# The MLPs of a two-layer hybrid encoder step: another order of the first up products, another order of the down products, resident weight halves loaded in steps

## The chip, the cores and the metric

The kernel runs on one core of a Trainium2 chip. The metric is the device time of one execution in microseconds (us); lower is better. A core has five engines that work at the same time, each through its own instructions in its own order, and wait for one another by semaphores: TensorE (PE in the profile, its weight loads PEld) for matrix products, VectorE (DVE), ScalarE (ACT) and GpSimd (POOL) for elementwise work, and SyncE (SP), which here only issues transfers (DMA) between the chip's memory (DRAM) and SBUF, the larger of the core's two on-chip memories. Products accumulate in the smaller one, PSUM, in banks. DMAs are issued from SP's queue and from POOL's queue.

## The reference, cut to what matters

The program is one inference step of a small encoder with two layers (`DEPTH = 2`, `D_MODEL = 1024`), over 1072 tokens: 16 meta tokens, 32 sample frames and 1024 prompt frames. Each layer has a mixer (attention and gated linear attention in layer 0, forgetting attention in layer 1) and then an MLP with a hidden width of 4096. The change touches the MLPs:

```python
def mlp(h, w_up, w_down):
    u = jax.nn.relu(h @ w_up)
    return (u * u) @ w_down
...
        xp = xp + mlp(rmsnorm(xp, norm_mlp[l]), w_up[l], w_down[l])
        xs = xs + mlp(rmsnorm(xs, norm_mlp[l]), w_up[l], w_down[l])
```

Everything is fp32.

## The kernel before

**fp32 as three products.** Each fp32 operand is split into a high part (a cast on ACT, line 64) and a low part (the rest, a subtraction, line 66 on DVE or line 68 on POOL, by the last argument of `hi_lo`). `mm3` then issues three products: high x high (line 75), high x low (76), low x high (77). In the profile a wait at line 75 is thus one for a high part, a wait at 76 one for the low part of the activations, a wait at 77 one for the low part of the weights.

**Seven products instead of eight.** Both matrix products of an MLP are done by a Strassen-Winograd scheme: each matrix is cut into 2 x 2 quadrants, and seven products of sums of quadrants make the result. The names are those of the scheme: A11, A12, A22, S1 to S4 are weights (S: sums of quadrants), B11, B21, B22, T1 to T4 activations (T: sums of quadrants). T1 is B12 - B11; T2 is B22 less T1 and needs T1 first; T3 is B22 - B12; T4 is B21 - T2.

**Layout.** `xT` holds the residual in SBUF, transposed: 128 partitions x 8 blocks of features x 1072 tokens. The tokens are cut into four quarters (`qs`) of 268 (layer 0) or 264 (layer 1). Quarters 0 and 1 are the left halves of B (B11: feature blocks 0 to 3, B21: 4 to 7), quarters 2 and 3 the right ones (B12, B22). One column index `c` (0 or 1) says which quarter of a half is meant, so a T1 of column 1 needs quarters 1 and 3.

**The norm ahead of it.** `mlp_norm(q)` normalizes quarter `q`: eight squares on ACT (134) with sums on DVE and POOL (136, 139), the mean over features as a product with a constant matrix (`normed`, 145), a Newton step (148 to 152) to 1/sqrt, and then eight multiplications in place, one for each feature block (878). `norm(cols, between)` issues the squares, then the steps handed in as `between`, then the rest, mean product included. `mlp_sums(q)` (884 on) then forms T1, T2, T3, T4 and B22 of this column, each with its high and low part into an `ho_` tile (`operand`). It is called for quarter 2 and, behind `mlp_norm(3)`, for quarter 3.

**The up product** (`up`) is a generator, one step a `yield`. It runs over 16 pairs `b` (a pair is 128 hidden units from either half) and, inside, over the seven products of `UP`: A11, A12, S1, S2, S3, A22, S4. A step makes two outputs (`c` = 0, 1) of 12 products each: 24 products. `ready(at)` makes the weights of four steps ahead: `up_load` loads a pair's raw weights (two DMAs of 512 KB into `mu_raw`, two buffers), `up_weights` forms sums and splits them into `mu_w` (five buffers). Results of a pair go, squared-ReLU and differences included (994, 1001, 1005), into eight slots laid over one half of `xT`, the halves taken in turn by even and odd pairs. Pair 0 keeps its first sum in `mu_early`, since `xT` is still being read at that time. When a pair is done, one DMA from POOL's queue stores seven of its slots to DRAM (`ud`, in four tiles of four pairs each; 1008). The last pair's store is kept back (`last_store`, 1093) until the down product has begun. `mlp` hands two up steps to `mlp_norm(3)` as `between`.

**The down product** (`down`) runs seven products of `DOWN` (`n`), each in two passes (`c`), each pass over 16 blocks `kb` of 12 products. `acts` loads the activations of two pairs from `ud` (SP's queue, 1067; three buffers `md_ur`) and splits them into `md_u` (four buffers), three groups ahead. `weights(n, kb)` makes the weights of a block in `md_w{kb}`, one buffer each, which is refilled in the pass `c` = 1 of the product before. Two halves of `w_down` quadrants stay in SBUF as `k1` and `k2`, 16 blocks each in four tiles of 1 MB; other quadrants are loaded block by block into `md_raw` (256 KB each, three buffers). Before the change, `k1` is loaded with A11 ahead of the first pass from SP's queue, and `k2` with A21 during the first pass, at blocks 2, 6, 10 and 14, from POOL's queue; each of these loads stands behind a one-element copy (`behind`, 1073) that waits for the activations of its block. S2 = A21 + A22 - A11 is the second product, so its weights (1041, 1042, then the split) are made during the second pass. At block 4 of the first four products the residual of the product's quadrant is loaded back into `xT` from `xsave` (1121, POOL's queue), and at the end of a pass the outputs in PSUM are added to it (1139). A product starts new sums in PSUM if `n` is in `first`; the others go on in the sums of the product before.

**What sets the order.** In `mlp` PE's order is that of the program (`manual_schedule` for PE), and in `down` the orders of SP and POOL are, too, up to the second product. All else, DVE and ACT throughout, is ordered by a planner that simulates the time line when the kernel is built.

## Time and profile before

| | us |
|---|---|
| time before, median of 3 runs | 2821.92 |
| the runs | 2826.71, 2821.92, 2815.38 |
| the profiled execution, its own time | 2817.04 |
| its span (first to last instruction) | 2815.3 |
| its mean granted TensorE clock | 0.969 of full speed |

The profile is of one execution; its span is 1.7 us shorter than the time of that execution. A row of its first part gives an engine's busy time, share of the span and count of instructions. Rows of the order in time give start, duration, engine, line, operation, what is written and what is read, and in brackets how long the engine was idle before and what ended the idling. Rows in which instructions are merged give their count as x2, x4 and so on. Rows of the waits give the time waited in all, how many times, and the longest wait. Rows of stretches give the bounds, the length, the busy time and count of PE, PEld, DVE, ACT and POOL, then the granted PE clock, the busy share of the DMA engines and GB/s. The MLP of layer 0 has its up product from 582 to 934 us and its down product from 934 to about 1285; that of layer 1 from 2102 to 2451 and from there to the end.

### The profile page before, as it was taken

The numbers are of one execution on the slowest core, as the hardware profiler recorded it, in microseconds if no ns is written. First come the engines' busy times: TensorE is split into PE (matmuls) and PEld (weight loads), VectorE is DVE, ScalarE is ACT, GpSimd is POOL, SyncE is SP. The second block draws the span as 40 slices with busy tenths as digits, with TensorE's granted clock in tenths as the row PEclk, the third lists the DMA queues.
The fourth block names the chain that finished last, engine by engine and source line by source line (L and its number), as shares of the span: only waits on it lengthen the run. The fifth ranks groups of instructions, "written<-read, shape, count | busy, mean of one in ns | idle before, by whom it ended". The sixth has DMA issues, their size and how long they took to land.

```text
span 2815.3 us, 49213 instructions
## 1 busy us (share of the span) xinstructions
PE 2624.8 (93%) x18391; PEld 2437.4 (87%) x18391; DVE 1892.2 (67%) x3850; ACT 1266.0 (45%) x2833; POOL 634.5 (23%) x693
## 2 busy tenths in 40 slices
PE   5899999869999999999999888999968999999998
PEld 5888988769999899998798766778868999999998
DVE  5934478786766686677634556778788767677553
ACT  4345465443333354545333356666653333335342
POOL 3423365110000211012201244555510000111000
PEclk9999999989999999999999989999989999999999
DMA  6343242225443766544464555444232344586643
GB/s 194 101 134 105 74 149 58 75 87 160 128 155 128 279 207 202 145 132 130 131 207 134 145 144 133 98 101 98 63 92 96 130 154 141 180 269 210 195 142 104
DMA packets 358038, 394.82 MB, mean 140 GB/s; under 512 B 41567, under 2 KB 294200, under 8 KB 355752
## 3 DMA queue, kind: packets, MB, share of 16 engines
q1 hardware_dynamic: 340840, 306.55, 38.2%
q0 software_dynamic: 16960, 85.13, 8.4%
q8 instruction: 145, 2.38, 0.4%
q14 instruction: 93, 0.76, 0.1%
HBM read 264.99 MB, written 125.48 MB: 139 GB/s over the span
## 4 chain that ended last, share of the span: by engine, by line
PE 75%; DVE 11%; DMA 4%; ACT 2%; issue 2%; POOL 1%; SPq 0%; DVEq 0%; ACTq 0%; POOLq 0%
PE bank L75 12%; PE bank L76 12%; PE bank L77 12%; PE mu_y L76 8%; PE mu_y L77 8%; PE mu_y L75 8%; PE bank L1490 3%; PE bank L1500 2%; PE bank L1501 1%; DMA md_ur<-ud 1%; PE fx_s L1472 1%; PE fx_s L1473 1%; PE bank L257 1%; DMA md_raw<-in_w_down 1%; DVE xT L878 1%
## 5 line engine op out<-in xcount | busy, mean ns | idle before, releaser
L75 PE MATMUL bank<-pj_wh,h 128*128 128x384 f32 (+3 forms) x832 | 300.1, 363 | 9.8 <-ACT pj_wh L64 7.4
L77 PE MATMUL bank<-pj_wh,h 128*128 128x384 f32 (+3 forms) x832 | 297.4, 359 | 6.1 <-DVE h L66 4.8
L76 PE MATMUL bank<-pj_wl,h 128*128 128x384 f32 (+3 forms) x832 | 298.5, 360 | 3.0 <-DVE pj_wl L66 2.9
L76 PE MATMUL mu_y<-md_u,md_w 128*128 128x268 f32 (+1 forms) x896 | 259.9, 290 | 13.3 <-DVE md_u L66 11.3
L77 PE MATMUL mu_y<-md_u,md_w 128*128 128x268 f32 (+1 forms) x896 | 259.4, 290 | 6.1 <-POOL md_w L68 6.1
L75 PE MATMUL mu_y<-md_u,md_w 128*128 128x268 f32 (+1 forms) x896 | 260.7, 291 | 0.3 <-ACT md_u L64 0.2
L75 PE MATMUL bank<-md_u,md_w 128*128 128x268 f32 (+1 forms) x896 | 257.3, 287 | 0.0
L76 PE MATMUL bank<-md_u,md_w 128*128 128x268 f32 (+1 forms) x896 | 255.9, 286 | 1.2 <-DVE md_u L66 1.2
L77 PE MATMUL bank<-md_u,md_w 128*128 128x268 f32 (+1 forms) x896 | 255.6, 285 | 0.0
L64 ACT CAST md_u<-md_ur 128x536 fp32r<-128x536 f32 (+1 forms) x224 | 141.6, 636 | 232.0 <-PE mu_y L77 119.6
L66 DVE TENSOR_TENSOR md_u<-md_ur,md_u 128x536 fp32r<-128x536 f32 (+1 forms) x220 | 155.3, 710 | 131.3 <-ACT md_u L64 131.1
L77 PE MATMUL mu_y<-ho_T,mu_w 128*128 128x268 f32 (+1 forms) x768 | 220.0, 286 | 0.0
L76 PE MATMUL mu_y<-ho_T,mu_w 128*128 128x268 f32 (+1 forms) x768 | 219.8, 286 | 0.0
L75 PE MATMUL mu_y<-ho_T,mu_w 128*128 128x268 f32 (+1 forms) x768 | 219.3, 286 | 0.0
L1303 POOL TENSOR_TENSOR fx_p<-fx_p,sm_den 128x144 f32<-128x144 f32 (+7 forms) x128 | 150.6, 1177 | 182.1 <-DVE sm_den L1302 166.6
L66 DVE TENSOR_TENSOR mu_w<-mu_raw,mu_w 128x512 fp32r<-128x512 f32 x160 | 109.6, 687 | 116.9 <-ACT mu_w L64 116.9
L76 PEld LDWEIGHTS mu_y<-md_u,md_w 128*128 128x128 f32 x896 | 172.4, 192 | 15.2 <-DVE md_u L66 12.8
L64 ACT CAST mu_w<-mu_raw 128x512 fp32r<-128x512 f32 x160 | 99.3, 622 | 190.6 <-PE bank L77 124.7
L75 PEld LDWEIGHTS bank<-pj_wh,h 128*128 128x128 f32 x832 | 160.2, 193 | 22.8 <-ACT pj_wh L64 7.9
L77 PEld LDWEIGHTS mu_y<-md_u,md_w 128*128 128x128 f32 x896 | 172.3, 192 | 6.5 <-POOL md_w L68 6.5
L77 PEld LDWEIGHTS bank<-pj_wh,h 128*128 128x128 f32 x832 | 159.8, 192 | 17.6 <-DVE h L66 5.1
L76 PEld LDWEIGHTS bank<-pj_wl,h 128*128 128x128 f32 x832 | 160.3, 193 | 15.9 <-DVE pj_wl L66 4.4
(553 smaller groups left out, 8156.4 us busy)
## 6 DMA issues: line engine op xcount, KB each, us to landing
md_raw<-in_w_down SPq DMA_DIRECT2D x160, 256.0 KB
mu_raw<-in_w_up SPq DMA_DIRECT2D x64, 512.0 KB
ud<-xT POOLq DMA_DIRECT2D x16, 1876.0 KB, 7.5
md_ur<-ud SPq DMA_DIRECT2D x112, 268.0 KB
ud<-xT POOLq DMA_DIRECT2D x16, 1848.0 KB, 10.0
md_ur<-ud SPq DMA_DIRECT2D x112, 264.0 KB
fh_ka<-zk SPq DMA_DIRECT2D x32, 260.0 KB
md_k<-in_w_down SPq DMA_DIRECT2D x8, 1024.0 KB
```

Source lines behind the costliest of these rows:

```text
L64: nc.scalar.copy(hi, src)
L66: nc.vector.tensor_tensor(lo, src, hi.bitcast(F32), op=ALU.subtract)
L75: mm(out, ah, bh, start=start, stop=False)
L76: mm(out, ah, bl, start=False, stop=False)
L77: mm(out, al, bh, start=False, stop=stop)
L257: nc.tensor.matmul(*args, start=k == x == 0, stop=k == KB - 1 and x == 1)
L878: nc.vector.scalar_tensor_tensor(x[:, k], x[:, k], self.gain[:, 2 * self.l + 1, k:k + 1], y, op0=ALU.mult, op1=ALU.mult)
L1303: nc.gpsimd.tensor_tensor(p[:, :n], p[:, :n], den[:, 0:1].to_broadcast([P, n]), op=ALU.mult)
L1472: nc.tensor.matmul(s[:, a:b], qa[:, qc], ka[:, t0 + a:t0 + b], start=True, stop=False)
L1473: nc.tensor.matmul(s[:, a:b], qb[:, qc], kb[:, t0 + a:t0 + b], start=False, stop=ma >= mb)
L1490: nc.tensor.transpose(pt[:m, P * j:P * j + P], pr[j][:, k0:k0 + m], self.ident)
L1500: nc.tensor.matmul(po[:, c], vt[:m, t], th[:m, c], start=t == 0, stop=False)
```

## The change

In the up product the order of steps starts with A11 and A12 of pair 0, then A11 and A12 of pair 1; then come the other five products of pair 0, then those of pair 1, then the pairs from 2 on as before. Pair 1 gets a `mu_early` of its own. `mlp` hands four steps instead of two to `mlp_norm(3)`. T1's difference and split move into a function `first_sum`, which for quarter 3 is issued behind the fourth of the eight multiplications of `mlp_norm`. `nm_t` has three buffers instead of four, but for the first norm of the program.

In the down product A12 comes first and A11 second; the rest keeps its order. `k2` is loaded first, with A12; `k1` gets A11 during the first product and `k2` gets A21 during the second, at the blocks listed in `later`, from POOL's queue behind the same kind of copy. So S2's weights are made one product later. The low parts at the start are all on DVE. Weights are made four blocks ahead instead of six in the first pass. Of the last pair, the square, the four differences and the store are issued one at a time in the first blocks of the first pass. The residual is loaded at block 6, and for the products 0, 2, 3 and 4.

```diff
--- before.py
+++ after.py
@@ -130,7 +130,7 @@
             e = at in (1, 3, 5)
             first = at < 2
             at += 1
-            sq = acc[e] if first else sb.tile([P, QMAX], F32, name="nm_t", bufs=4)[:, :w]
+            sq = acc[e] if first else sb.tile([P, QMAX], F32, name="nm_t", bufs=3)[:, :w]
             nc.scalar.activation(sq, x[:, k], AF.Square)
             if not first:
                 (nc.gpsimd if e else nc.vector).tensor_tensor(acc[e], acc[e], sq, op=ALU.add)
@@ -213,7 +213,7 @@
         few = TILES[0][1] if first else 0
         for k in range(KB):
             g = self.gain[:, n, k:k + 1]
-            t = sb.tile([P, w], F32, name="nm_t", bufs=4)[:, :w - few]
+            t = sb.tile([P, w], F32, name="nm_t", bufs=3 if n else 4)[:, :w - few]
             nc.vector.scalar_tensor_tensor(t, x[:, k, few:], g, y[:, few:], op0=ALU.mult, op1=ALU.mult)
             self.hi_lo(t, hi[:, k, few:], lo[:, k, few:], "g" if k % 2 else "v")
         if few:
@@ -876,9 +876,18 @@
         x = self.xT[:, :, c0:c1]
         for k in range(KB):
             nc.vector.scalar_tensor_tensor(x[:, k], x[:, k], self.gain[:, 2 * self.l + 1, k:k + 1], y, op0=ALU.mult, op1=ALU.mult)
+
+            if q == 3 and k == 3:
+                self.first_sum(q)
         if q < 2:
             for n, name in enumerate(("B11", "B21")):
                 self.operand(name, x[:, 4 * n:4 * n + 4], q)
+
+    def first_sum(self, q):
+        (a0, a1), (c0, c1) = self.qs[q - 2], self.qs[q]
+        b11, b12 = self.xT[:, 0:4, a0:a1], self.xT[:, 0:4, c0:c1]
+        self.nc.vector.tensor_tensor(b11, b12, b11, op=ALU.subtract)
+        self.operand("T1", b11, q)
 
 
     def mlp_sums(self, q):
@@ -886,8 +895,8 @@
         (a0, a1), (c0, c1) = self.qs[q - 2], self.qs[q]
         b11, b21 = (self.xT[:, k:k + 4, a0:a1] for k in (0, 4))
         b12, b22 = (self.xT[:, k:k + 4, c0:c1] for k in (0, 4))
-        sub(b11, b12, b11)
-        self.operand("T1", b11, q)
+        if q == 2:
+            self.first_sum(q)
         sub(b11, b22, b11)
         self.operand("T2", b11, q)
         sub(b12, b22, b12)
@@ -942,10 +951,12 @@
         slot = {x: n + 1 for n, x in enumerate(self.STORED)}
         slot["B12"] = 0
         tt, stt = nc.vector.tensor_tensor, nc.vector.scalar_tensor_tensor
-        todo = [(b, n) for b in range(self.NP) for n in range(7)]
+
+        todo = [(b, n) for b in range(2) for n in range(2)] + [(b, n) for b in range(2) for n in range(2, 7)]
+        todo += [(b, n) for b in range(2, self.NP) for n in range(7)]
         pairs, ws = {}, {}
 
-        early = sb.tile([P, hw], F32, name="mu_early", bufs=1)
+        early = [sb.tile([P, hw], F32, name=f"mu_early{b}", bufs=1) for b in range(2)]
         self.ud = [self.dram.tile([P, 4, 7, hw], F32, name=f"ud{self.l}{g}") for g in range(4)]
 
         def ready(at):
@@ -974,7 +985,7 @@
                 for k in range(4):
                     self.mm3(out, (w[:, 0, k], w[:, 1, k]), (act[:, 0, k, cc], act[:, 1, k, cc]), first and k == 0, k == 3, wn in ("S2", "S3", "A22", "S4"))
                 u = {x: y[:, cc] for x, y in v.items()}
-                u1 = early[:, cc] if b == 0 else u["B11"]
+                u1 = early[b][:, cc] if b < 2 else u["B11"]
                 if wn == "A11":
                     nc.scalar.copy(u1, out)
                 elif wn == "A12":
@@ -994,26 +1005,25 @@
                 stt(x, src, 0.0, src, op0=ALU.max, op1=ALU.mult)
 
             if wn == "S1":
-                squared(v["B11"], early if b == 0 else v["B11"])
+                squared(v["B11"], early[b] if b < 2 else v["B11"])
             elif wn == "S3":
                 squared(v["B22"], v["B22"])
             elif wn == "A22":
                 tt(v["B21"], v["B21"], v["B21"], op=ALU.mult)
             elif wn == "S4":
-                squared(v["B12"], v["B12"])
+                self.last = [partial(squared, v["B12"], v["B12"])]
                 for x, p, m in (("T1", "B12", "B11"), ("T2", "B22", "T1"), ("T3", "B22", "B12"), ("T4", "B21", "T2")):
-                    tt(v[x], v[p], v[m], op=ALU.subtract)
-                store = partial(nc.gpsimd.dma_start, self.ud[b // 4][:, b % 4], place[:, b % 2, 1:8, :hw])
-                if b < self.NP - 1:
-                    store()
-                else:
-                    self.last_store = store
+                    self.last.append(partial(tt, v[x], v[p], v[m], op=ALU.subtract))
+                self.last.append(partial(nc.gpsimd.dma_start, self.ud[b // 4][:, b % 4], place[:, b % 2, 1:8, :hw]))
+
+                while b < self.NP - 1 and self.last:
+                    self.last.pop(0)()
                 del pairs[b]
             yield
 
 
-    DOWN = (("A11", "B11", ("11",)), ("S2", "T2", ("12",)), ("S3", "T3", ("22",)), ("A22", "T4", ("21",)),
-            ("A12", "B21", ("11",)), ("S1", "T1", ("22", "12")), ("S4", "B22", ("12",)))
+    DOWN = (("A12", "B21", ("11",)), ("A11", "B11", ("11",)), ("S2", "T2", ("12",)), ("S3", "T3", ("22",)),
+            ("A22", "T4", ("21",)), ("S1", "T1", ("22", "12")), ("S4", "B22", ("12",)))
 
 
     def down(self, k1, k2, sb, ps, mid, done):
@@ -1037,6 +1047,8 @@
             a, b = (k[kb // 4][:, kb % 4] for k in (k1, k2))
             if x == "A11":
                 src = a
+            elif x == "A12":
+                src = b
             elif x == "S2":
                 tt(b, b, raw("A22", kb), op=ALU.add)
                 tt(b, b, a, op=ALU.subtract)
@@ -1065,7 +1077,7 @@
             t = sb.tile([P, 2, QMAX], F32, name="md_ur", bufs=3)[:, :, :qw]
             hl = sb.tile([P, 2, 2, QMAX], F32R, name="md_u", bufs=4)[:, :, :, :qw]
             nc.sync.dma_start(t, self.ud[g // 2][:, 2 * (g % 2):2 * (g % 2) + 2, s, qw * c:qw * c + qw])
-            self.hi_lo(t, hl[:, 0], hl[:, 1], "g" if (n, c) == (0, 0) and g < 2 else "v")
+            self.hi_lo(t, hl[:, 0], hl[:, 1])
             return hl
 
 
@@ -1084,18 +1096,20 @@
 
         order = ExitStack()
         order.enter_context(self.tc.manual_schedule(engines={mybir.EngineType.SP, mybir.EngineType.Pool}))
-        load(k1[0], "A11", 0, 4)
+        load(k2[0], "A12", 0, 4)
         ready(0)
         for x in range(1, 4):
-            load(k1[x], "A11", 4 * x, 4)
-        for kb in range(6):
-            w[0, kb] = weights(0, kb, "g" if kb < 3 else "v")
-        self.last_store()
+            load(k2[x], "A12", 4 * x, 4)
+
+        later = {(0, 0, 10): (k1[0], "A11", 0), (0, 0, 14): (k1[1], "A11", 4), (0, 1, 2): (k1[2], "A11", 8), (0, 1, 6): (k1[3], "A11", 12),
+                 (1, 0, 4): (k2[0], "A21", 0), (1, 0, 8): (k2[1], "A21", 4), (1, 0, 12): (k2[2], "A21", 8), (1, 1, 0): (k2[3], "A21", 12)}
+        for kb in range(4):
+            w[0, kb] = weights(0, kb)
         at = 0
         out = {}
         for n, c in passes:
             x, _, to = self.DOWN[n]
-            first = n in (0, 4, 5, 6)
+            first = n in (0, 1, 5, 6)
             if (n, c) == (1, 0):
                 order.close()
             if first:
@@ -1105,14 +1119,17 @@
                     ready(at)
                     u = us.pop(todo[at])
                     at += 1
-                if n == 0 and c == 0 and kb + 6 < NP:
-                    w[0, kb + 6] = weights(0, kb + 6)
-                if n == 0 and c == 0 and kb % 4 == 2:
-                    x = k2[kb // 4]
+                if n == 0 and c == 0 and kb + 4 < NP:
+                    w[0, kb + 4] = weights(0, kb + 4)
+
+                if self.last:
+                    self.last.pop(0)()
+                if (n, c, kb) in later:
+                    x, name, k = later[n, c, kb]
                     behind(x[0:1, 0, 0:1], u)
-                    load(x, "A21", kb - 2, 4, nc.gpsimd)
-
-                if n < 4 and kb == 4:
+                    load(x, name, k, 4, nc.gpsimd)
+
+                if n in (0, 2, 3, 4) and kb == 6:
                     c0, c1 = self.qs[2 * (int(to[0][1]) - 1) + c]
                     f = 4 * (int(to[0][0]) - 1)
                     for k in range(f, f + 4, 2):
@@ -1122,7 +1139,7 @@
                 for ob in range(4):
                     f = slice(P * ob, P * ob + P)
                     hl = w[n, kb]
-                    self.mm3(out[c][ob], (hl[:, 0, f], hl[:, 1, f]), (u[:, 0, kb % 2], u[:, 1, kb % 2]), first and kb == 0, kb == NP - 1, n in (1, 2, 3))
+                    self.mm3(out[c][ob], (hl[:, 0, f], hl[:, 1, f]), (u[:, 0, kb % 2], u[:, 1, kb % 2]), first and kb == 0, kb == NP - 1, n in (2, 3, 4))
                 if c == 1 and n < 6:
                     w[n + 1, kb] = weights(n + 1, kb)
 
@@ -1155,7 +1172,7 @@
             with tc.tile_pool(name="mu", bufs=1, reuse_waits="tile") as sb:
                 steps = self.up(sb, ps)
                 self.mlp_sums(2)
-                self.mlp_norm(3, [partial(next, steps) for _ in range(2)])
+                self.mlp_norm(3, [partial(next, steps) for _ in range(4)])
                 self.mlp_sums(3)
                 for _ in steps:
                     pass
@@ -1163,7 +1180,7 @@
             ks = ExitStack()
             kp = pool(ks, "mk", "right")
 
-            k2, k1 = ([kp.tile([P, 4, 512], F32, name=f"md_k{x}{y}") for y in range(4)] for x in (2, 1))
+            k1, k2 = ([kp.tile([P, 4, 512], F32, name=f"md_k{x}{y}") for y in range(4)] for x in (1, 2))
             sb = pool(st, "md")
             if self.l:
                 self.so = pool(st, "so", bufs=2)
```

## The prediction

> **What bounds the kernel now.** I read the page first, then TensorE's (PE's) waits, then the order in time of each engine around the places that these waits name.
>
> ```profile
> span 2815.3 us, 49213 instructions
> ...
> PE 2624.8 (93%) x18391; PEld 2437.4 (87%) x18391; DVE 1892.2 (67%) x3850; ACT 1266.0 (45%) x2833; POOL 634.5 (23%) x693
> ...
> PE 75%; DVE 11%; DMA 4%; ACT 2%; issue 2%; POOL 1%; SPq 0%; DVEq 0%; ACTq 0%; POOLq 0%
> ```
>
> ```profile
> PE bank L75 <- ACT ho_T L64: 20.9, 2, 10.6
> ...
> PE mu_y L76 <- DVE md_u L66: 11.3, 6, 2.7
> ...
> PE mu_y L77 <- POOL md_w L68: 6.1, 2, 3.1
> ...
> PE bank L76 <- DVE ho_T L66: 3.8, 2, 1.9
> ```
>
> ```profile
> 880.00:904.00 24.00, 24.00 (x197) 24.00 (x196) 15.29 (x27) 8.02 (x17) 0.53 (x1) 1.00 0.54 185
> ```
>
> PE sets the end: 93% busy, 75% of the chain. The change leaves its products as many as they are, so it can win only what PE idles in the MLPs, and the slow clock behind idling. In the wait rows (us in total, times, longest) T1 costs 20.9 + 3.8 us, once in each of the two up products; the start of the down products and their operands cost 11.3 + 6.1. The last row, a stretch of 24 us with the busy time (and count) of PE first and the granted clock behind POOL's, prices PE: 197 products, 0.122 us each. An up step (24 products) is 2.92 us, a block of a down pass (12 products) 1.46 us, a pass of 16 blocks 23.4 us.
>
> **Part 1, up product.** PE's order is written by hand: `norm` puts the mean's product (L145) behind the steps given to it, formerly two, now four. Layer 0, in time:
>
> ```profile
> 592.86 0.61 PE L145 MATMUL bank<-nm_acc,mean 128*128 128x268 f32 x2
> 595.35 0.43 ACT L150 ACTIVATE nm_a<-nm_y 128x268 f32<-128x268 f32 x1
> 596.75 0.68 DVE L66 TENSOR_TENSOR mu_w<-mu_raw,mu_w 128x512 fp32r<-128x512 f32 x1
> 598.55 0.43 DVE L151 SCALAR_TENSOR_TENSOR nm_a<-bank,nm_a 128x268 f32<-128x268 f32 x1
> 599.49 3.36 DVE L878 SCALAR_TENSOR_TENSOR xT<-xT,gain,nm_y 128x268 f32<-128x268 f32 x8
> 602.76 1.27 DVE L889 TENSOR_TENSOR xT<-xT 128x1072 f32<-128x1072 f32 x1
> 604.06 1.09 ACT L64 CAST ho_T<-xT 128x1072 fp32r<-128x1072 f32 x1
> 605.20 0.59 PE L75 MATMUL bank<-ho_T,mu_w 128*128 128x268 f32 x1 [10.25 <-ACT ho_T L64]
> 607.70 0.59 PE L76 MATMUL bank<-ho_T,mu_w 128*128 128x268 f32 x1 [1.90 <-DVE ho_T L66]
> ...
> 2126.91 0.59 PE L75 MATMUL bank<-ho_T,mu_w 128*128 128x264 f32 x1 [10.61 <-ACT ho_T L64]
> ```
>
> From the mean's product to T1's high part are 12.3 us, to its low part 14.8. The two added steps do not fill this gap: they stand ahead of L145 and move it to 592.86 + 5.85 = 598.7. What shrinks is the chain. ACT ends its three at 595.78, 2.9 us behind L145. DVE then came 2.8 us late, being busy with weights of pair 1; the added 5.85 us let it finish those, so I cost this at nothing. L151 and L152 take 0.94, four blocks instead of eight 1.68, the difference 1.24, the cast 1.2: T1's high part is there 8.0 us after L145, at 606.7. DVE does the other four blocks (1.68) beside the cast, then the low part (1.27): 608.5. That is 0.8 later than 607.70, with 5.85 us more work done: a gain of **5.0**. PE still idles some 6 us, so the slow restart stays. T2 is next: difference, cast and low part end near 612, and PE, at half speed through 24 products, wants it near 613.5.
>
> Bounds: if DVE stays late by 2.8, the gain is 2.3. If pair 1's first weights also come when they did (596.75 + 0.68, while PE now wants them at 592.9), 4.6 more is lost: -2.3. Above, 5.5. Layer 1's wait, 10.61, is the same. Two layers: **10**, from -4.6 to 11. The fewer `nm_t` buffers, the second `mu_early` and the swapped tiles I cost at nothing: six squares are added in another engine's shadow.
>
> **Part 2, start of the down product.** Formerly three low parts of weights and two of operands were POOL's; now DVE makes all.
>
> ```profile
> 934.45 0.43 DVE L990 TENSOR_TENSOR xT<-xT,bank 128x268 f32<-128x268 f32 x1 [1.04 <-PE bank L77]
> 934.58 3.07 POOL L68 TENSOR_TENSOR md_u<-md_ur,md_u 128x536 fp32r<-128x536 f32 x2 [14.57 <-ACT md_u L64]
> 934.92 1.55 DVE L994 SCALAR_TENSOR_TENSOR xT<-xT 128x536 f32<-128x536 f32 x1
> 935.95 0.39 PE L76 MATMUL mu_y<-md_u,md_w 128*128 128x268 f32 x1 [1.01 <-POOL md_u L68]
> 936.50 6.85 DVE L1005 TENSOR_TENSOR xT<-xT 128x536 f32<-128x536 f32 x4
> 939.40 0.59 PE L77 MATMUL mu_y<-md_u,md_w 128*128 128x268 f32 x1 [3.06 <-POOL md_w L68]
> 943.65 0.56 POOL L1093 DMA_DIRECT2D ud<-xT  x1 [0.87 <-DVE xT L1005]
> 944.50 7.30 DVE L66 TENSOR_TENSOR md_w<-md_k,md_w 128x512 fp32r<-128x512 f32 x12
> 952.49 0.39 PE L76 MATMUL mu_y<-md_u,md_w 128*128 128x268 f32 x1 [2.12 <-DVE md_u L66]
> 968.24 0.43 DVE L1139 TENSOR_TENSOR xT<-xT,mu_y 128x268 f32<-128x268 f32 x1 [0.27 <-PE mu_y L77]
> ```
>
> The same stretch in other views: L1005's shortest, median and longest in ns; the clock behind the third wait; the store's time to landing (shortest, median, longest); two operand loads of the chain.
>
> ```profile
> L1005 DVE TENSOR_TENSOR xT<-xT x128: 694/705/1792, 626.4 to 2458.3; 128x536 f32<-128x536 f32 x64, 128x528 f32<-128x528 f32 x64
> ...
> 952.00:956.00 4.00, 3.51 (x20) 3.51 (x21) 1.15 (x2) 0.80 (x2) 0.00 (x0) 0.74 1.04 380
> ...
> DMA to landing us min/median/max: 7.0/7.2/7.5
> ...
> 945.14 10.60 DMA md_ur<-ud
> ...
> 957.25 5.78 DMA md_ur<-ud
> ```
>
> Beside POOL's work each of pair 15's four differences (L1005) takes 1.71 us, against a median of 0.705. The first pass runs from 934.4 to 968.2: 33.8 us for 23.4 of products. Lost are 10.4: 1.01 + 3.06 + 2.12 of waits and 4.2 of slow clock (its column reads 0.74 behind the third).
>
> New sum, three waits. First, DVE's low parts of one operand and one weight: 1.4 (0.7 if one is early; 4.9 if the square and four differences, now 3.5 without POOL, stay ahead). Second, block 6 wants the fourth operand: PE is there 8.8 + 1.4 after 934.4; DVE by then has 3 operands (2.1), 16 weights at 7.30/12 (9.7) and the 3.5 queued, which end at 950.2 if the operand stands behind all of them, so 0 to 5.6; I take the middle, 2.8. Third, the last store. Its six instructions, the store on POOL's queue and the quarter loads behind it, are now issued block by block. It cannot be issued before 938.4 nor, by that count, after 950.2; I take 943. It lands 7.2 later, pair 12's operand 5.8 to 10.6 after that, then 1.4 for cast and low part: 957.4, for block 12 wanted at 956.2: 1.2 (ends: 0 and 13). The waits make 5.4, and I leave 1 for the clock: 6.4 lost instead of 10.4, a gain of **4**, from -7 to 9.7. Two layers: **8**, from -14 to 19.
>
> Rule against row: the Trainium skill, "SBUF — State Buffer", section "SBUF: two separate sides", calls the port pair of DVE and GpSimd an exclusive lock whose loser fully blocks; 1.71 against 0.705 agrees. [...] Here a POOL issue inside DVE's run from 944.50 (the first row of the next fence) took 0.79 us; by the row the sum stands. [...]
>
> Queues: the quarter loads of A11 and A21 now stand on POOL's queue, six to sixteen blocks ahead of their casts, each behind a copy that waits for its block's operand. Queued behind such a copy are only the next quarter and the residual's loads, wanted by L1139 at a pass's end. Six blocks are 8.8 us.
>
> ```profile
> 944.92 0.79 POOL L1027 DMA_DIRECT2D md_k<-in_w_down  x1 [0.30 <-POOL md_k L1073]
> ...
> md_k<-in_w_down POOLq DMA_DIRECT2D x4, 1024.0 KB, 9.4
> ```
>
> They land in 9.4 us, at most about a us late on ACT; behind ACT stand operands made two groups (5.8 us) ahead, so PE sees nothing.
>
> **Part 3, S2's weights a pass later.** They cost DVE three instructions each for 16 blocks beside operands:
>
> ```profile
> L1041 DVE TENSOR_TENSOR md_k<-md_k,md_raw x16: 681/683/694, 971.4 to 1005.5; 128x512 f32<-128x512 f32 x16
> ...
> 971.38 0.69 DVE L1041 TENSOR_TENSOR md_k<-md_k,md_raw 128x512 f32<-128x512 f32 x1 [1.05 <-DMA md_raw<-in_w_down]
> ...
> 976.00:1000.00 24.00, 21.20 (x164) 20.25 (x162) 23.22 (x40) 11.17 (x19) 1.64 (x5) 1.00 0.69 212
> 1000.00:1024.00 24.00, 22.24 (x179) 22.05 (x178) 18.75 (x33) 8.63 (x14) 3.26 (x8) 1.00 0.61 178
> ...
> 2496.00:2520.00 24.00, 20.94 (x170) 20.52 (x169) 24.00 (x43) 9.76 (x17) 1.97 (x6) 1.00 0.77 235
> ```
>
> DVE is full, and PE (second column) idles 2.80 + 1.76 and 3.06 us: 7.6. The work is the same in its new place; but there DVE need not begin with a wait for raw weights behind a store and four quarter loads. I take half, **3.8**, between 7.6 and, as the same crowding could be worse by half, -3.8.
>
> **Sum.** 10 + 8 + 3.8 = 22 us off the profiled execution's 2817.04: 2795. That execution lies 4.9 below the median 2821.92 of the runs shown (2815.38 to 2826.71); on the median's footing I forecast **2800**. About 0.5%, 14 us, is what a measurement here can tell from no change.
>
> **Rivals.** *Half given back*, 2814: the planner, not the text, orders DVE and ACT; DVE stays 2.8 late before L151 and the fourth operand stands behind all sixteen weights. Then up brings 2 x 2.3, the start 2 x 1, S2 1.4. For it: the twelve weights in a row from 944.50. Against: without POOL that run starts earlier. *Slower*, 2840: the late store. If square and differences fall behind the weights, the store goes out near 950; layer 0 loses from a store later than about 943 to 948 on (968.2 less four blocks, 1.4, a load and 7.2). Priced at the bounds, -7 and, from the same early weights in the up product, -2.3 a layer: 18.6. For it: the spread steps are issued behind weights. Against: they are ready as early as 934.9. *Everything covered*, 2785: up 11, start 18, S2 7.6. *Clock*: in the rows, 2.12 us of idling was followed by 0.74, while the waits of 976 to 1024 left 1.00. The Trainium skill, "TensorE: Matmul & The Clock Gate", section "What's actually happening", puts the drop at an idle window of about 3.4 us; by it the start would keep full speed and the sum be 2 us better, which changes no case.
>
> **How the numbers follow.** Forecast 0.48 (its own range 2790 to 2810), everything covered 0.12, half given back 0.26, slower 0.14. Faster by over 0.5% is below 2807.8: 0.9 of the first, the second, a tenth of the third: 0.58. Slower is above 2836: most of the last, 0.13. Within: 0.29. The range 2782 to 2828 cuts off the slower case's core and a little of the best.
>
> **What would show it.** In the new profile: PE's wait for T1 near 6 and 1.5 us (not 10.3 and 1.9), L151 straight behind L150; no low part on POOL, L1005 near 0.7 everywhere; the last store before 944 and no PE wait for a DMA-late operand around block 12; DVE full one pass later. Wrong would be: a PE wait for pair 1's weights ahead of L145, the store behind the weights, or new waits around S2's new pass.

## The result and the profile after

The changed kernel took 2798.09 us (median of four runs, 2795.57 to 2799.56), beside 2819.06 for the kernel before (four runs): a ratio of 0.9922 with a 95% interval from 0.9907 to 0.9936. In a later session, beside eleven runs of the kernel before, it took 2801.35 us, a ratio of 0.9938 (0.9924 to 0.9951). So the change is worth 0.6 to 0.8%, some 17 to 21 us. The forecast was 2800.

First the page of the changed kernel: span, busy time of the engines, and the chain that ended last by engine.

```profile
span 2795.3 us, 49150 instructions
...
PE 2622.7 (94%) x18377; PEld 2440.8 (87%) x18391; DVE 1886.4 (67%) x3860; ACT 1265.2 (45%) x2833; POOL 628.1 (22%) x699
...
PE 77%; DVE 10%; DMA 3%; issue 2%; ACT 2%; POOL 1%; SPq 0%; DVEq 0%; ACTq 0%; POOLq 0%
```

All engines do what they did (PE was busy for 2624.8 us before). What became less is idling between products, and the slow clock behind it. PE's waits, the rows that answer to those of before:

```profile
PE bank L75 <- ACT ho_T L64: 14.6, 2, 7.8
...
PE mu_y L76 <- DVE md_u L66: 13.0, 2, 6.5
...
PE bank L76 <- DVE ho_T L66: 3.8, 2, 1.9
```

The wait for T1's high part fell from 20.9 to 14.6 us. The waits for low parts made by POOL (6.1 us) are gone. Those for the down product's operands (11.3 us, six times) became 13.0 us in only two waits, one at either start of a down product. Where each piece lies is seen when the span is cut at PE's first product with `ho_B`, its first with `md_u`, and its last. These are the rows for layer 0, first before, then after:

```profile
582.28 0.59 PE L75 MATMUL mu_y<-ho_B,mu_w 128*128 128x268 f32 x1 [4.96 <-ACT mu_w L64]
...
934.55 0.39 PE L75 MATMUL mu_y<-md_u,md_w 128*128 128x268 f32 x1
...
1285.85 0.28 PE L77 MATMUL bank<-md_u,md_w 128*128 128x268 f32 x1
```

```profile
580.08 0.59 PE L75 MATMUL mu_y<-ho_B,mu_w 128*128 128x268 f32 x1 [5.16 <-ACT mu_w L64]
...
928.67 0.39 PE L75 MATMUL mu_y<-md_u,md_w 128*128 128x268 f32 x1
...
1272.48 0.28 PE L77 MATMUL bank<-md_u,md_w 128*128 128x268 f32 x1
```

Differences of such rows, taken alike in all traces, give the table to which the experiments refer (us, one profiled execution each; the last column is the median of all runs, but for the kernel before, whose medians in the four sessions were 2818 to 2819):

| kernel | up, layer 0 | down 0 | up 1 | down 1 | both MLPs | rest of span | median |
|---|---|---|---|---|---|---|---|
| before | 352.3 | 351.6 | 348.7 | 356.3 | 1408.8 | 1406.5 | 2819.06 |
| changed | 348.6 | 344.1 | 346.4 | 353.8 | 1392.9 | 1402.4 | 2798.09 |
| changed, again | 349.0 | 345.4 | 346.4 | 353.0 | 1393.8 | 1409.8 | 2801.35 |
| up alone | 348.6 | 349.4 | 345.9 | 356.1 | 1400.0 | 1403.5 | 2811.03 |
| down alone | 352.2 | 344.1 | 348.7 | 351.8 | 1396.8 | 1409.2 | 2805.29 |
| mean behind two steps | 347.8 | 343.2 | 346.0 | 352.6 | 1389.6 | 1405.0 | 2795.94 |
| start by hand | 348.9 | 341.9 | 346.1 | 353.3 | 1390.1 | 1406.6 | 2796.72 |
| before, SyncE's order shorter | 352.6 | 345.5 | 347.4 | 354.1 | 1399.5 | 1410.7 | 2810.34 |
| SyncE's order longer | 348.6 | 345.5 | 346.5 | 352.3 | 1392.9 | 1409.1 | 2801.65 |
| low parts on GpSimd | 350.1 | 343.8 | 346.1 | 353.1 | 1393.1 | 1402.2 | 2802.36 |
| first sum by hand | 351.8 | 344.0 | 348.0 | 352.2 | 1396.0 | 1409.7 | 2807.94 |
| start by hand, two steps | 350.3 | 339.1 | 346.5 | 350.5 | 1386.4 | 1405.3 | 2790.34 |
| all sums by hand | 349.0 | 343.8 | 346.7 | 350.9 | 1390.4 | 1409.7 | 2797.20 |
| both by hand | 347.4 | 339.5 | 347.6 | 352.2 | 1386.7 | 1402.9 | 2791.84 |

Two things have to be read off it first. The span fell by 20.0 us, the two MLPs by 15.9: 5.9 in the up products, 10.0 in the down products. And "rest of span" runs from 1402 to 1411 over these kernels; two executions of the changed one gave 1402.4 and 1409.8. So the remaining 4.1 us are no more than what executions of one kernel differ by, and a difference of a few us between two medians must be looked for in the MLP columns before it is believed. These too scatter: the up product of layer 0 took 348.6 to 350.3 us in six executions that run the same instructions there (both of the changed kernel, start by hand with one and with two steps, SyncE's order longer, low parts on GpSimd).

**The up product after.** The T1 chain of layer 0, from the order in time of each engine:

```profile
596.06 0.61 PE L145 MATMUL bank<-nm_acc,mean 128*128 128x268 f32 x2
598.26 0.44 DVE L151 SCALAR_TENSOR_TENSOR nm_a<-bank,nm_a 128x268 f32<-128x268 f32 x1 [0.24 <-ACT nm_a L150]
599.21 3.36 DVE L878 SCALAR_TENSOR_TENSOR xT<-xT,gain,nm_y 128x268 f32<-128x268 f32 x8
602.48 1.27 DVE L889 TENSOR_TENSOR xT<-xT 128x1072 f32<-128x1072 f32 x1
603.72 1.28 DVE L66 TENSOR_TENSOR ho_B<-xT,ho_B 128x1072 fp32r<-128x1072 f32 x1
603.78 1.08 ACT L64 CAST ho_T<-xT 128x1072 fp32r<-128x1072 f32 x1
604.92 0.59 PE L75 MATMUL bank<-ho_T,mu_w 128*128 128x268 f32 x1 [6.76 <-ACT ho_T L64]
606.09 2.51 DVE L66 TENSOR_TENSOR ho_T<-xT,ho_T 128x1072 fp32r<-128x1072 f32 x2
607.42 0.59 PE L76 MATMUL bank<-ho_T,mu_w 128*128 128x268 f32 x1 [1.91 <-DVE ho_T L66]
```

L151 stands right behind ACT now: DVE's lateness of 2.8 us is gone. But the row of L878 has x8 ahead of L889: the planner ran all eight multiplications ahead of the difference that the text puts behind the fourth. Behind the difference come B22's low part (`ho_B`) and T3's difference (L902, at 604.91), and only then T1's low part, the first of the two at 606.09. That is the order of the kernel before. With the call moved behind the eighth one, the planner makes the very same order on all five engines, so that part of the change did nothing.

**The down product's start after**, layer 0, rows of PE, DVE and POOL, then two stretches behind the wait (the clock stands behind POOL's busy time):

```profile
929.03 0.72 DVE L1005 SCALAR_TENSOR_TENSOR xT<-xT 128x536 f32<-128x536 f32 x1
929.78 2.72 DVE L1126 TENSOR_TENSOR xT<-xT 128x536 f32<-128x536 f32 x4
932.42 2.49 DVE L66 TENSOR_TENSOR md_w<-md_k,md_w 128x512 fp32r<-128x512 f32 x4
933.03 0.53 POOL L1126 DMA_DIRECT2D ud<-xT  x1 [18.89 <-ACT md_w L64]
934.83 1.96 DVE L66 TENSOR_TENSOR md_u<-md_ur,md_u 128x536 fp32r<-128x536 f32 x3
935.59 0.59 PE L76 MATMUL mu_y<-md_u,md_w 128*128 128x268 f32 x1 [6.53 <-DVE md_u L66]
```

```profile
936.00:938.00 2.00, 2.00 (x11) 2.00 (x11) 2.00 (x5) 0.00 (x0) 0.00 (x0) 0.50 1.02 360
...
942.00:944.00 2.00, 2.00 (x18) 2.00 (x17) 2.00 (x5) 0.32 (x1) 2.00 (x1) 1.00 0.00 0
```

The planner put the square, all four spread differences and four weights ahead of the operands' low parts, so that PE stands for 6.53 us at its second kind of product. The four differences take 2.72 us in place of 6.85, since POOL no longer computes beside them, and the store leaves 4.4 us behind the first product. After this wait the clock is at half until about 941, and the pass runs through. It takes 33.2 us, against 34.6 before.

**S2's weights after.** One line's instructions (first and last start behind the durations):

```profile
L1053 DVE TENSOR_TENSOR md_k<-md_k,md_raw x16: 679/684/694, 990.9 to 1026.8; 128x512 f32<-128x512 f32 x16
```

They begin 42 us ahead of the first S2 pass (its first product is at 1033.3); before, 24 us (971.4 for a pass that began at 995.0). All passes from the second to the ninth now take 23.8 us in layer 0; before, the second took 25.9 and the third 27.8. In layer 1 the third fell from 27.0 to 23.4.

### The profile page after: what moved, and what is told of

Its sections match the earlier page's. It is cut to its first block, busy times and chain, and to the rows that moved or that the text cites. A ratio compares the mean times of both kernels' runs of the same rounds, so it can differ in the third digit from the quotient of the medians.

```text
span 2795.3 us, 49150 instructions
## 1 busy us (share of the span) xinstructions
PE 2622.7 (94%) x18377; PEld 2440.8 (87%) x18391; DVE 1886.4 (67%) x3860; ACT 1265.2 (45%) x2833; POOL 628.1 (22%) x699
## 4 chain that ended last, share of the span: by engine, by line
PE 77%; DVE 10%; DMA 3%; issue 2%; ACT 2%; POOL 1%; SPq 0%; DVEq 0%; ACTq 0%; POOLq 0%
PE bank L75 13%; PE bank L76 12%; PE bank L77 12%; PE mu_y L77 8%; PE mu_y L76 8%; PE mu_y L75 8%; PE bank L1507 3%; PE bank L1517 2%; PE bank L1518 1%; PE fx_s L1489 1%; PE bank L257 1%; PE fx_s L1490 1%; DMA md_raw<-in_w_down 1%; DVE xT L878 1%; PE bank L1214 1%
## 5 line engine op out<-in xcount | busy, mean ns | idle before, releaser
L76 PEld LDWEIGHTS mu_y<-md_u,md_w 128*128 128x128 f32 x896 | 172.5, 193 | 13.5 <-DVE md_u L66 13.4
```

The costliest lines, as they stand in the source:

```text
L76: mm(out, ah, bl, start=False, stop=False)
```

## The experiments

Line numbers shift by up to a dozen in some variants; the operations named are the same.

### Up alone and down alone

The first keeps the kernel before and takes the up product's edits, the second the down product's:

```diff
+        todo = [(b, n) for b in range(2) for n in range(2)] + [(b, n) for b in range(2) for n in range(2, 7)]
+        todo += [(b, n) for b in range(2, self.NP) for n in range(7)]
...
-                self.mlp_norm(3, [partial(next, steps) for _ in range(2)])
+                self.mlp_norm(3, [partial(next, steps) for _ in range(4)])
```

> Only the up product's part of the change (step order, four steps ahead of the mean, second mu_early, first_sum, nm_t buffers); the down product is that of before. Theory (the two parts add): PE's wait for T1 falls from 10.3 and 10.6 us to about 6.8 and 7.8, each up product from 352.2 and 348.7 us to about 348.6 and 346.5, the down product keeps its waits (1.0, 3.1, 2.1 and those of S2). Time some 6 us under before, up to 10 if the 4 us gained outside the MLPs hang on this part. Rival (the gain sits in the down product, and the new order of the up product only moves PE's idling): within 2 us of before.

```diff
-    DOWN = (("A11", "B11", ("11",)), ("S2", "T2", ("12",)), ("S3", "T3", ("22",)), ("A22", "T4", ("21",)),
+    DOWN = (("A12", "B21", ("11",)), ("A11", "B11", ("11",)), ("S2", "T2", ("12",)), ("S3", "T3", ("22",)),
...
-        for kb in range(6):
-            w[0, kb] = weights(0, kb, "g" if kb < 3 else "v")
-        self.last_store()
+        for kb in range(4):
+            w[0, kb] = weights(0, kb)
```

> Only the down product's part of the change; the up product is that of before. Theory: one wait of about 6.5 us for the low part of the first operand in place of three, no waits around S2's weights, first three passes shorter by 1.4 + 2.1 + 4.0 us in layer 0 and 1.1 + 0 + 3.6 in layer 1; time 10 to 13 us under before. T1's wait stays at 10.3 and 10.6. Rival (S2's waits went because the earlier end of the up product shifted everything): the waits at S2, 4.6 and 3.1 us, are back and the time is within 5 us of before.

Measured: 2811.03 us, ratio 0.9968 (0.9955 to 0.9982), and 2805.29, 0.9949 (0.9931 to 0.9966). In the table the parts hardly touch each other: up alone has the up products of the changed kernel (348.6 and 345.9), with down products within 2.2 us of those of before, and down alone has the up products of before (352.2 and 348.7) and the changed kernel's down products within 2 us. The parts are worth 6.5 us (up) and 12.0 us (down) in these traces, 5.9 and 10.0 in the whole.

### The mean behind two steps

The changed kernel with two steps of `up` ahead of the mean's product, not four, so that T1's chain starts two steps earlier:

```diff
-                self.mlp_norm(3, [partial(next, steps) for _ in range(4)])
+                self.mlp_norm(3, [partial(next, steps) for _ in range(2)])
```

> The changed kernel, but with two steps ahead of the mean's product and the two steps of pair 1 behind it, where they fill PE's wait. Theory (the wait is the length of the chain behind the mean's product, and steps ahead of it do not fill it): T1's wait falls from 6.8 and 7.8 us to 3 to 4.5 each, time 4 to 8 us under the changed kernel. Rival (the four steps are worth having ahead because DVE is still full when ACT has finished): the chain grows by what it gains, from 8.9 us back to 12 or more, T1's wait stays near 7 and the time is that of the changed kernel.

Measured: 2795.94 us, ratio 0.9915 (0.9895 to 0.9936); the up products together 693.8 us against 695.0, which is within their scatter. From the start of the up product, the mean's product came 5.8 us earlier and T1's low part only 0.8. DVE, layer 0:

```profile
599.48 3.35 DVE L878 SCALAR_TENSOR_TENSOR xT<-xT,gain,nm_y 128x268 f32<-128x268 f32 x8
602.75 0.42 DVE L992 TENSOR_TENSOR mu_early<-mu_early,bank 128x268 f32<-128x268 f32 x1
...
604.03 0.68 DVE L66 TENSOR_TENSOR mu_w<-mu_raw,mu_w 128x512 fp32r<-128x512 f32 x1
604.64 1.26 DVE L889 TENSOR_TENSOR xT<-xT 128x1072 f32<-128x1072 f32 x1
```

Between the eighth multiplication and T1's difference the planner put the outputs and weights of pair 1, 1.9 us, and more of them ahead of the multiplications. So T1's wait is set by DVE's whole line up to the difference and not by the place of the mean's product.

### T1's difference in the order of the text, and all sums so

Since the planner had ignored the early call, DVE's order was written by hand: first for the eight multiplications, T1's difference and T1's low part, then on through the low parts of T2, T3, T4 and B22.

```diff
+        hand = ExitStack()
+        if q == 3:
+            hand.enter_context(self.tc.manual_schedule(engines={mybir.EngineType.DVE}))
         for k in range(KB):
             nc.vector.scalar_tensor_tensor(x[:, k], x[:, k], self.gain[:, 2 * self.l + 1, k:k + 1], y, op0=ALU.mult, op1=ALU.mult)
             if q == 3 and k == 3:
-                self.first_sum(q)
+                self.first_diff(q)
+        if q == 3:
+            self.operand("T1", self.xT[:, 0:4, self.qs[1][0]:self.qs[1][1]], q)
+        hand.close()
...
```

> The changed kernel with VectorE's order written by hand in the multiplications of the fourth quarter's norm: four blocks, T1's difference, the other four blocks, T1's low part; in the changed kernel the planner ran all eight blocks ahead of the difference. Theory (the early sum's term of the forecast was lost to the planner's order, and the wait for T1 is this chain): the high part of T1 comes 1.7 us earlier (four multiplications of 0.42) and the low part 2.3 earlier; the waits ahead of T1's first two products, 8.7 us in layer 0 and 9.7 in layer 1, fall by 2.0 to 2.5 each, the up products, 348.6 and 346.5 us, shorten by as much, and the time is 4 to 5 us under the changed kernel, 2793 to 2794. Rival (T2 and the sums behind it come next, so that what T1 gives up is waited for there): T1's waits fall as said, waits of 1.5 to 2.5 us appear ahead of T2's products, and the up products stay within 0.7 us; 2797 to 2799.

Measured: 2807.94 us, ratio 0.9965 (0.9951 to 0.9979): slower than the changed kernel, by 3.1 us in the MLP columns. PE, layer 0:

```profile
609.08 0.59 PE L75 MATMUL bank<-ho_T,mu_w 128*128 128x268 f32 x1 [5.25 <-ACT ho_T L64]
610.78 0.59 PE L76 MATMUL bank<-ho_T,mu_w 128*128 128x268 f32 x1 [1.11 <-DVE ho_T L66]
...
619.12 0.39 PE L76 MATMUL mu_y<-ho_T,mu_w 128*128 128x268 f32 x1 [3.27 <-DVE ho_T L66]
```

T1's two waits fell as said, from 8.67 to 6.36 us, and T2's low part is now waited for 3.27 us, with a slow clock behind it: the up products are 3.2 and 1.6 us longer than in the changed kernel. The planner, free behind the hand-written stretch, had put T3's difference and B22's low part ahead of T2's difference, and four more instructions between that and T2's low part. That is the rival, and worse.

In the second run the hand order goes on through `mlp_sums(3)`, closed behind B22's low part (`self.hand.close()`).

> As the run with the first sum by hand, but VectorE's order is by hand through all the sums of the fourth quarter: four blocks, T1's difference, four blocks, T1's low part, then difference and low part of T2, of T3, of T4, and B22's low part. With the hand order on T1 alone, T1's waits had fallen from 8.7 to 6.4 us and from 9.7 to 7.3, but the planner then put B22's low part and T3's difference ahead of T2's low part, which PE waited for 3.3 and 2.5 us. Theory (VectorE's line is what PE waits for, in whatever order it stands; in the order of use the gain on T1 stays): T1's waits stay at 6.4 and 7.3 within 0.5, T2's fall under 1 us, and the up products take 345.5 to 347.0 and 343.5 to 345.0 us, 4 to 5 us less than the changed kernel's 348.6 and 346.5 together. Rival (in the strict order VectorE now stands idle for ScalarE's cast ahead of each low part, 1.1 us a sum): waits of 2 us and more appear ahead of T3's or T4's products, and the up products stay at 348 to 351 and 346 to 349.

Measured: 2797.20 us, ratio 0.9923 (0.9910 to 0.9935); up products 349.0 and 346.7 us, no gain. ACT and PE, layer 0 (L1006 is the copy that takes S2's result out of PSUM, L994 in the changed kernel):

```profile
617.14 1.09 ACT L64 CAST ho_T<-xT 128x1072 fp32r<-128x1072 f32 x1 [1.42 <-DVE xT L912]
618.13 0.37 ACT L1006 COPY xT<-mu_y 128x268 f32<-128x268 f32 x1
...
622.17 0.39 PE L75 MATMUL mu_y<-ho_T,mu_w 128*128 128x268 f32 x1 [1.86 <-ACT xT L1006]
```

T2's low part is in time now, and so are T3's and T4's. PE waits 0.41 and 1.86 us ahead of T3's products, for a copy on ACT that stands behind T3's and T4's casts (2.29 in layer 1). The up products and the waits are where the rival had them, but it is ACT's line that PE waits for, not a low part. What T1 gives up (2.3 us) is asked for again by the next step in each order that was tried, by DVE or by ACT. An order by hand for ACT as well was not tried, so it stays open whether these 2.3 us are to be had at all.

### The start of the down product by hand

The changed kernel with DVE's order in the program's, too, up to the second product, so that the first operands' low parts go first and the spread steps stand between the weights:

```diff
-        order.enter_context(self.tc.manual_schedule(engines={mybir.EngineType.SP, mybir.EngineType.Pool}))
+        order.enter_context(self.tc.manual_schedule(engines={mybir.EngineType.SP, mybir.EngineType.Pool, mybir.EngineType.DVE}))
```

> The changed kernel, but DVE's order, too, is that of the program while the first product of the down product runs, so that the low parts of the first operands and weights stand ahead of the last pair's square and differences. Theory (the prediction's first wait was undersized because the planner put the square, four differences and four weights ahead): the first wait falls from 6.5 us to about 1.5, the clock stays up, the first pass takes 26 to 29 us instead of 33.2, and the time is 6 to 12 us under the changed kernel. Rival (the last store then comes late, as the slower rival of the prediction has it): the store goes out 3 to 8 us later, PE waits that much at block 12, and the time is within 3 us of the changed kernel.

Measured: 2796.72 us, ratio 0.9918 (0.9900 to 0.9935), 1.4 us below the changed kernel: on the rival's side. Yet the theory's mechanism is in the trace. PE and POOL, both layers:

```profile
933.98 0.39 PE L76 MATMUL mu_y<-md_u,md_w 128*128 128x268 f32 x1 [0.61 <-DVE md_u L66]
935.84 0.59 PE L77 MATMUL mu_y<-md_u,md_w 128*128 128x268 f32 x1 [1.47 <-DVE md_w L66]
946.39 0.53 POOL L1126 DMA_DIRECT2D ud<-xT  x1 [27.94 <-issue]
959.48 0.39 PE L75 MATMUL mu_y<-md_u,md_w 128*128 128x268 f32 x1 [1.34 <-ACT md_u L64]
...
2464.67 0.42 PE L75 MATMUL mu_y<-md_u,md_w 128*128 128x264 f32 x1 [3.13 <-ACT md_u L64]
```

The wait of 6.53 us became 0.61 + 1.47. But the store now leaves 13.4 us behind the first product (4.4 in the changed kernel), and its reader is late: the operand of pairs 14 and 15, 1.9 us in layer 0 and 3.5 in layer 1 with its low part. The expectations call this place block 12; by the count of PE's products it is block 14. The load of these two pairs was issued at 953.29, as the store landed (946.39 + 6.8); that of pairs 12 and 13 had gone out at 941.57. In layer 1 that is a second long wait and a second spell of slow clock: its first pass takes 35.4 us, 2.5 longer than in the changed kernel, while layer 0's takes 30.7, 2.5 shorter. One cure, one new wait.

The next run lets two of the spread steps go with each block, so that the store follows the third block's weights and not the sixth's:

```diff
-                if self.last:
-                    self.last.pop(0)()
+                for _ in range(2):
+                    if self.last:
+                        self.last.pop(0)()
```

> The kernel with VectorE's order by hand at the down product's start, with one more edit: the spread steps are issued two behind each block of the first pass in place of one, so that the store follows the third block's weights and not the sixth's. In the run with one step a block the first wait had fallen from 6.5 to 2.1 us in both layers, the store was issued 12 to 13 us later than in the changed kernel, and block 12 waited 1.9 us in layer 0 and 3.5 in layer 1, with a slow clock behind it. Theory (block 12's wait is the late store's, handed on through the load of the last pairs): the store is issued about 3 us earlier, the waits at block 12 fall under 0.5 us in layer 0 and under 1 in layer 1, the first waits stay at 2 to 3, and the first passes take 28 to 30 us (30.7 and 35.4 with one step, 33.2 and 32.9 in the changed kernel); down products together 8 to 11 us shorter than the changed kernel's 697.9, and 2788 to 2792. Rival (the operand is late by the traffic of that stretch, whenever the store went): the waits at block 12 stay at 1.5 to 3.5 us, the first passes stay within 1 us of 30.7 and 35.4, and 2795 to 2798.

Measured: 2790.34 us, ratio 0.9902 (0.9887 to 0.9918), beside 0.9938 (0.9924 to 0.9951) for the changed kernel against the same runs; the two intervals do not touch. PE and POOL, both layers:

```profile
934.65 0.39 PE L76 MATMUL mu_y<-md_u,md_w 128*128 128x268 f32 x1 [0.62 <-DVE md_u L66]
936.51 0.39 PE L77 MATMUL mu_y<-md_u,md_w 128*128 128x268 f32 x1 [1.46 <-DVE md_w L66]
944.48 0.53 POOL L1127 DMA_DIRECT2D ud<-xT  x1 [25.37 <-issue]
...
2458.57 0.39 PE L75 MATMUL mu_y<-md_u,md_w 128*128 128x264 f32 x1 [0.59 <-ACT md_u L64]
```

The store leaves 10.8 us behind the first product. Block 14 does not wait in layer 0 and waits 1.2 us in layer 1 (0.59 and two shorter ones). The first passes take 28.1 and 29.4 us, the down products 689.6 together, 8.3 less than the changed kernel's. The theory holds, and no version has a lower median (the run of both by hand below is as fast within its interval). In that run the store left as early, and layer 1 waited 2.7 us; yet the operand was no later. Its cast starts 24.7 us behind the first product there and 24.6 here. PE's clock stayed full there, so that PE came to block 14 some 1.4 us sooner and waited that much longer.

### The low parts on GpSimd again

```diff
-            self.hi_lo(t, hl[:, 0], hl[:, 1])
+            self.hi_lo(t, hl[:, 0], hl[:, 1], "g" if (n, c) == (0, 0) and g < 2 else "v")
...
-            w[0, kb] = weights(0, kb)
+            w[0, kb] = weights(0, kb, "g" if kb < 3 else "v")
```

> The changed kernel with the low parts of the first three blocks of weights and of the first two operand pairs of the down product computed by GpSimd again, as before the change. Theory (the forecast's: GpSimd's differences and VectorE's get into each other's way there, as in the profile before, where the square of that stretch took 1.74 us in place of 0.70): the first wait of the down product, 6.5 us in the changed kernel, grows to 8 to 10, and the two first passes, 33.2 and 32.9 us, by 2 to 4 each; 2801 to 2806. Rival (what makes the first wait is VectorE's line of a square, four differences and four weights ahead of the operands' low parts, so that work taken off that line helps): the first wait falls to 2 to 5, the first passes get 1 to 3 us shorter each, 2792 to 2796.

Measured: 2802.36 us, ratio 0.9946 (0.9925 to 0.9967): the changed kernel's time. POOL, DVE and PE, layer 0:

```profile
933.78 5.17 POOL L68 TENSOR_TENSOR md_w<-md_k,md_w 128x512 fp32r<-128x512 f32 x3
932.68 6.85 DVE L1126 TENSOR_TENSOR xT<-xT 128x536 f32<-128x536 f32 x4
932.12 0.39 PE L76 MATMUL mu_y<-md_u,md_w 128*128 128x268 f32 x1 [1.01 <-POOL md_u L68]
935.58 0.59 PE L77 MATMUL mu_y<-md_u,md_w 128*128 128x268 f32 x1 [3.07 <-POOL md_w L68]
948.67 0.39 PE L76 MATMUL mu_y<-md_u,md_w 128*128 128x268 f32 x1 [1.43 <-DVE md_u L66]
```

Both theories are half right. The two engines do get into each other's way (1.71 us a difference in place of 0.68), and work taken off DVE's line does help its other work. Three waits of 5.5 us in all stand where one of 6.53 stood, and the first passes take 32.8 and 34.0 us beside 33.2 and 32.9. Moving the low parts to DVE brought nothing while the spread differences and weights stood ahead of them.

### How long SyncE's order is kept by hand

In the kernel before, SyncE's and GpSimd's hand order ends one pass earlier; in the changed kernel, one product later:

```diff
-            if (n, c) == (1, 0):
+            if (n, c) == (0, 1):
```

> The kernel before with one edit: the hand order of SyncE and GpSimd at the start of the down product ends one pass earlier, ahead of (0,1) in place of (1,0), so that the planner may place the loads of S2's raw blocks and of the operands of the second and third pass. In the profile before, the second and third pass of layer 0 took 25.9 and 27.8 us and the third of layer 1 took 27.0, against 23.8 and 23.3 for a pass without a wait: 2.1 + 4.0 + 3.7 = 9.8 us too long in all. Theory (SyncE's fixed order keeps operand loads behind raw loads that wait for a buffer): these three lengths fall to 24 to 24.5 and 23.5, and the time is 7 to 10 us under the kernel before on the same chip, about 2810. Rival (the DMA traffic of the first pass, or the place of S2 in the second pair of passes, makes the operands late): the three lengths stay within 1 us of what they were, and the time is that of the kernel before within 2 us. A fall of half of it, 3 to 6 us, would say that both take part.

```diff
-            if (n, c) == (1, 0):
+            if (n, c) == (2, 0):
```

> The changed kernel with one edit: the hand order of SyncE and GpSimd ends one pass pair later, ahead of (2,0) in place of (1,0), so that S2's first raw loads (issued in the second pass of A11) again stand between operand loads in the order of the program. Theory (SyncE's fixed order): the third and fourth passes or the one behind them, 23.8 us each in layer 0 now, grow by 4 to 6 us together in layer 0 and by 3 to 4 in layer 1, and waits for the operands' low parts come back; 2804 to 2808. Rival (traffic or place): each of these passes stays within 0.7 us, the waits stay away, and the time is that of the changed kernel within 2 us, 2796 to 2800.

Measured: 2810.34 us, ratio 0.9968 (0.9954 to 0.9982), and 2801.65, 0.9941 (0.9922 to 0.9961). The first is the theory: the passes of 25.9 and 27.8 us in layer 0 and of 27.0 in layer 1 take 23.8, 23.8 and 23.4 (layer 1's second grew by 1.9), and the down products fall by 8.3 us. The second is its rival: with the raw loads again between operand loads in a fixed order, one pass of 24.8 us is all that came back (S2's in layer 0, with a wait of 0.75 us); the changed kernel's second execution has one of 24.9, a pass earlier. What agrees with both runs is when S2's weights begin. First the shorter order in the kernel before, then the longer one in the changed kernel:

```profile
L1041 DVE TENSOR_TENSOR md_k<-md_k,md_raw x16: 683/690/704, 960.2 to 998.5; 128x512 f32<-128x512 f32 x16
```

```profile
L1053 DVE TENSOR_TENSOR md_k<-md_k,md_raw x16: 679/686/695, 1009.2 to 1044.8; 128x512 f32<-128x512 f32 x16
```

The S2 passes begin at 995.9 and 1037.1 us there: leads of 36 and 28 us, and no long wait. The kernel before had a lead of 24 us and 4.6 us of waits in layer 0, the changed kernel one of 42 and none. The other traces agree: leads of 23 to 25 us (both layers of the kernel before and of up alone) go with 3.1 to 3.4 us of waits in the S2 pass, 28 and 29 us (the longer order) with 0.75 and 0, and 36 us or more, in all others, with none. Two stretches of 36 us from the start of these weights show the difference, first before, then with the shorter order:

```profile
971.00:1007.00 36.00, 31.43 (x244) 30.30 (x243) 32.81 (x56) 14.72 (x25) 2.42 (x6) 1.00 0.75 238
```

```profile
963.00:999.00 36.00, 36.00 (x291) 35.86 (x290) 32.94 (x57) 16.05 (x27) 6.66 (x13) 1.00 0.89 295
```

DVE does the same 33 us of work in 36 us in both; PE (the second column) stood for 4.57 us of the first and none of the second. Sixteen blocks of three instructions at 0.684 us are 32.8 us of DVE, more than a pass of 23.8 holds. A lead of 24 us makes them compete with the operands of the pass that uses them; 28 hardly did. Operand loads were late as well in the kernel before: PE wanted a low part at 1000.2 us whose load landed just ahead of its cast at 1000.49. What DVE's line and the late loads cost each was not told apart.

### Both by hand, and the changed kernel again

> The edits of the two runs beside it together: all sums of the fourth quarter and the start of the down product in VectorE's order by hand, spread steps two behind a block. If both theories hold and the stages are independent, the up products are those of the run with all sums by hand and the down products those of the run with two steps, each within 1 us, and the time is 2783 to 2788. If the sums' rival holds, it is the time of the run with two steps or up to 4 us above it; if the start's rival holds too, it is no better than the changed kernel.

Measured: 2791.84 us, ratio 0.9905 (0.9892 to 0.9918). All sums and the start by hand together are the start by hand alone: 1386.7 us in the MLPs against 1386.4, as for the case that the sums' rival holds.

> The changed kernel once more, nothing edited. In its first profile the two MLPs account for 15.8 of the 20.0 us by which its span is shorter (1408.8 to 1393.0), and the stages outside them for 4.2 (1406.5 to 1402.3). In the profiles of eight variants those outer stages took from 1402.2 to 1410.7 us, though what runs ahead of the first MLP is the same sequence in several of them. If that is scatter between executions, the two MLPs take 1393.0 within 1.5 us again and the outer stages anything from 1402 to 1411, most likely 1404 to 1409, and the median over rounds is 2799 to 2803. If the outer stages' 4.2 us belong to the changed order, they take 1402.3 within 1 us again and the median stays at 2797 to 2799.

Measured: 2801.35 us. The MLPs repeat within 0.9 us (1393.8), the rest of the span took 1409.8: scatter, as in the first of the two cases.

## Why the prediction was right, and what in it was not

The time came out 2 us beside the forecast, in part by luck: terms that were off went both ways. Inside the MLPs 15.9 of the 22 us came, and 4.1 us of the profiled span lie outside them, where executions of one kernel differ by more; the second session gave 2801.35.

**What bounds it**: right. PE's work stayed as it was, and what was gained beyond scatter is idling and slow clock inside the MLPs.

**Part 1, 10 us forecast, 5.9 measured.** DVE's lateness before L151 vanished in layer 0, at the price of nothing, as forecast. The step that failed is the order of DVE behind it, "four blocks instead of eight" and "DVE does the other four blocks (1.68) beside the cast, then the low part (1.27)". It was read off the text, while the planner, which the same prediction names as the one that orders DVE, ran eight and then two more instructions (603.72 to 606.09) ahead of T1's low part. From L151 to the end of that low part the forecast has 6.8 us; it took 9.1 (598.26 to 607.36), 2.3 more. L151 came 2.2 and not 2.9 us behind L145, which gave 0.7 back: 5.0 - 2.3 + 0.7 = 3.4, and layer 0's two T1 waits fell by 3.5 (12.15 to 8.67). In the run with T1's order by hand T1's waits fell by the same 2.3 us (8.67 to 6.36), but its up product grew longer: PE wants T2 "near 613.5" only as long as T1 is late. In layer 1 of the changed kernel, DVE was still some 1.2 us late before L151, and 2.3 were left of its up product.

**Part 2, 8 us forecast, 2.5 measured** (first passes 34.6 to 33.2 and 34.0 to 32.9). The failed step is the first wait: taken at 1.4, bounded at 4.9, measured 6.53. The order behind the bound was the right one, square and differences first, but four weights went ahead of the operands as well. The wait at block 6 (2.8) did not come, since PE got there 18.3 us behind its first product and not 10.2, past the fourth operand's low part (943.93). The one at block 12 (1.2) did not, since the store left early, at 4.4. The clock cost 33.2 - 6.5 - 23.8 = 2.9 us, not 1. The late store's mechanism is real: the run with DVE's order by hand shows it, at 1.9 and 3.5 us, and the next run nearly takes it away; but it acts at block 14, on the load of the last two pairs, not on "pair 12's operand". The first pass before was 34.6 us long, not the 33.8 of the sum: the row at 968.24 adds only the first of its finished outputs.

**Part 3, 3.8 us forecast, about 9 measured** (2.1 + 4.0 in layer 0, 3.6 in layer 1, less 0.8 in the new place). The mechanism, weights that need not begin with a wait for raw blocks behind other loads, was named; its size was halved for want of evidence, and the upper bound, 7.6, was nearer, as it counted the waits in three stretches and not the whole passes.

**Lost elsewhere**: the thirteenth pass of layer 1 took 31.7 us after 30.3. It took 29.8 to 32.7 in the other runs, so this is not shown to be the change's. **Rivals**: half given back (2814), slower (2840) and everything covered (2785) did not come as whole cases. But the planner, on which the first two rested, is what ate more than half of parts 1 and 2 (8.4 of 18 us came).

## What to carry to other kernels

An edit of the text moves work only on engines whose order is the text's: where a planner sets the order, compare the instruction orders of the two kernels first, and count a step that isn't in them as nothing. A wait in a chain through two engines is worth only what the next step in line can do without, so price the second wait too, and look on each engine for it. Work that overfills one pass needs a lead and not another place: count its time on the engine, compare with the pass, and start it that much earlier.
